# Mixer values normalized in the sample stage and streamed back by channel group

## The chip, the cores and the metric

The kernel runs on one core of a Trainium2 chip. The metric is the device time of one execution in microseconds (us), the median of several runs. PE is the matrix engine (TensorE), DVE the vector engine, ACT the scalar engine, POOL GpSimd, SP the engine that mostly issues DMAs. Each engine works through its own list of instructions in a fixed order, and waits where an operand or a buffer isn't ready.

## The reference, cut to what matters

One step of a two-layer decoder, for 1024 prompt tokens and a sample group of 64 tokens (8 sequences of 8) with 512 cached keys each. Layer 0 is what matters here:

```python
z = rms_norm(x, norm_g) @ w_in
zq, zk, zv, ga, zu, zvb, gb = jnp.split(z, cuts, axis=-1)
...
o_a = o.reshape(b, l, W_A) * jax.nn.silu(ga)                 # attention, gated
u = jax.nn.gelu(zu, approximate=False)
vb = layer_norm(jax.nn.gelu(zvb, approximate=False), ln_g, ln_b)
mixed = chunk_spatial(vb.reshape(b, l, G_B, CG_B), sp_w, sp_b).reshape(b, l, W_B)
o_b = u * mixed * jax.nn.silu(gb)                            # the mixer, gated
y = x + jnp.concatenate([o_a, o_b], axis=-1) @ w_out
```

`chunk_spatial` multiplies, for each of 8 channel groups of 128 and each chunk of 128 tokens, the values by a lower triangular 128x128 matrix over positions, and adds a bias per position. `layer_norm` is over the 1024 channels of a token: subtract the mean, multiply by the inverse deviation, by `ln_g` (per channel), add `ln_b` (per channel). The sample group's `vb` is an output. Layer 1 and the output projections aren't touched.

## The kernel before, in words

Tokens stand in 9 row tiles (8 of 128 prompt tokens, one of 64 sample tokens), or, transposed, in three column chunks (`CH`: 384, 384 and 320 columns). A projection is three matmuls per product (high by high, low by high, high by low part of the operands; `mm3`, L148 to L150), eight contraction tiles each: 24 matmuls.

Four stages of layer 0 follow each other:

- The head attention of the prompt (0 to 516 us). Its tail (516 to 572 us) still holds the last head's work, and between it the first `NPRE` = 8 of 24 gate units.
- A gate unit `gate_a(h, n)` (L240 to L256) is one head and one column chunk: it loads the attention output `oTr` from the DRAM buffer `oT_d` (ACT's queue, L248), does 24 matmuls into the PSUM tile `ga`, tanh on ACT (L250), one DVE operation (L251), the product on POOL (L254), and stores the result back into `oT_d` (ACT's queue, L255).
- The sample stage (572 to 816 us) is the attention of the 8 sample sequences over cached pages: key page transposes `ktp` (L536), whose PSUM tiles are copied to `kT` by DVE and ACT in turn (L537), then scores `ssc`, `ap`, values `sop`, and `sot`. Between its steps stands a list called `fill`: 16 gate units, and then 36 units `vb_unit` (L610 to L623), which project the mixer's values (`zv`: 4 column groups by 9 row tiles), copy them out (`zs`) and store them in the DRAM buffer `vb_d`. Key pages have 2 PSUM buffers, value pages (`vp`) 6 SBUF buffers.
- The mixer stage (816 to 1036 us): 24 units `b_dense` (48 matmuls into `zu` and `gb`, then Gelu, tanh, and products), each followed `ML` = 5 units later by `b_mix` (3 matmuls `mx` of the values with the position matrix, an addition of the bias `sbc` on DVE at L759, and the product `ob`). In its first steps `vb_norm` (L705 to L723) loads each of the nine row tiles from `vb_d`, takes Gelu on ACT (L712), statistics on DVE (L717) and POOL (L135, L136: inverse deviation), and two DVE operations (L720, L721) that apply mean and `ln_g`, and deviation and `ln_b`. All nine tiles stay in SBUF.

The code is written stage by stage. A scheduler with a cost model then sets the order in which each engine finds its instructions; DMAs go out in the order in which their issuing engine finds them, and hold that engine's later work back while they wait.

Of the kernel before, what the change touches and what calls it, by code (L numbers as in the profile page):

```python
# [23 lines left out]
NT = 9  # L24
# [12 lines left out]
NPRE = 8  # L37
# [18 lines left out]
ML = 5  # L56
# [20 lines left out]
def hybrid_step(  # L77
# [31 lines left out]
    vb_d = dram.tile([T + NS, D], F32, name="vb_d")  # L109
    v_d = dram.tile([T, D], F32, name="v_d")  # L110
# [77 lines left out]
    if True:  # L188
# [53 lines left out]
        def gate_a(h, n, new):  # L242
            load_gate(h)
            wh, wl = Wg[h]
            c0, cw = CH[n]
            pw_ = min(cw, SEQ - c0)
            mp, oT, g2 = new(h, n)
            nc.scalar.dma_start(oT[:, :pw_], oT_d[h][:, c0:c0 + pw_])  # L248
            mm3(mp[:, :cw], [(wh[k], wl[k], xh[n][:, k, :], xl[n][:, k, :]) for k in range(KT)])
            act.activation(g2[:, :cw], mp[:, :cw], AF.Tanh, scale=0.5)  # L250
            dve.scalar_tensor_tensor(g2[:, :cw], g2[:, :cw], 1.0, mp[:, :cw], ALU.add, ALU.mult)  # L251
            if n == 2:
                pool.tensor_copy(g2s[:, h, :], g2[:, pw_:cw])
            pool.tensor_tensor(oT[:, :pw_], oT[:, :pw_], g2[:, :pw_], ALU.mult)  # L254
            nc.scalar.dma_start(oT_d[h][:, c0:c0 + pw_], oT[:, :pw_])  # L255
            load_gate(h + 1)  # L256
# [249 lines left out]
        with ExitStack() as p15:  # L506
# [108 lines left out]
            def vb_unit(c, i):  # L615
# [6 lines left out]
                if i == NT - 1:  # L622
                    load_vb(c + 1)  # L623

            fill = [lambda h=h, n=n: gate_a(h, n, gate_tiles) for h, n in du[NPRE:]]
            fill += [lambda c=c, i=i: vb_unit(c, i) for c in range(4) for i in range(NT)]
# [41 lines left out]
        with ExitStack() as p2:  # L668
            pb = p2.enter_context(tc.tile_pool(name="pb", bufs=1, reuse_waits="tile"))
            vb = [pb.tile([P, D], F32, name=f"vb{i}") for i in range(NT)]  # L670

            lng = pb.tile([P, D], F32, name="lng")
            lnb = pb.tile([P, D], F32, name="lnb")
            nc.sync.dma_start(lng, ln_v_g.broadcast_to([P, D]))
            nc.sync.dma_start(lnb, ln_v_b.broadcast_to([P, D]))
# [10 lines left out]
            def mix_setup():  # L686
                for hh in range(2):
# [3 lines left out]
                    dve.tensor_copy(wT[:, hh * 4:hh * 4 + 4, :].rearrange("p g t -> p (g t)"), tp)  # L691
                tp = ps2.tile([P, 512], F32, tag="t", name="bdp", bufs=2)
# [11 lines left out]

            def vb_norm(i):  # L705
                r = rows(i)
                nc.sync.dma_start(vb[i][:r], vb_d[i * P:i * P + r, :])
                if i == NT - 1:
                    vx = pb.tile([P, D], F32, tag="ob", name="vx", bufs=1)
                    nc.sync.dma_start(vx[:r], vb_d[T:, :])  # L710
                    dve.tensor_tensor(vb[i][:r], vb[i][:r], vx[:r], ALU.add)
                act.activation(vb[i][:r], vb[i][:r], AF.Gelu)  # L712
                bst = pb.tile([P, 2, 6], F32, tag="bst", name=f"bst{i}", bufs=2)
                mv = pb.tile([P, 2], F32, tag="mv", name=f"mv{i}", bufs=2)
                rv = pb.tile([P, 1], F32, tag="lrv", name=f"lrv{i}", bufs=2)
                for q in range(2):
                    dve.bn_stats(bst[:r, q, :], vb[i][:r, q * 512:(q + 1) * 512])  # L717
                dve.bn_aggr(mv[:r], bst[:r].rearrange("p a b -> p (a b)"))
                rsqrt(rv[:r], mv[:r, 1:2], 1, 1.0)
                dve.scalar_tensor_tensor(vb[i][:r], vb[i][:r], mv[:r, 0:1], lng[:r], ALU.subtract, ALU.mult)  # L720
                dve.scalar_tensor_tensor(vb[i][:r], vb[i][:r], rv[:r], lnb[:r], ALU.mult, ALU.add)  # L721
                if i == NT - 1:
                    nc.sync.dma_start(vb_sample.rearrange("e b t d -> (e b t) d"), vb[i][:r])  # L723
# [7 lines left out]
            def b_dense(g, n):  # L731
# [7 lines left out]
                u = pb.tile([P, 384], F32, tag="u", name=f"u{g}_{n}", bufs=7)  # L739
# [7 lines left out]
            def b_mix(g, n, u):  # L747
# [6 lines left out]
                for q in range(nfull):  # L754
                    pe.matmul(mx[:, q * P:(q + 1) * P], vb[n * 3 + q][:, g * P:(g + 1) * P], wT[:, g, :], start=True, stop=True)
                mxs = pb.tile([P, 384], F32, tag="mxs", name=f"mxs{g}_{n}", bufs=2)
                if n == 2:
                    pe.matmul(mx[:, 256:320], vb[NT - 1][:NS, g * P:(g + 1) * P], bd[:, g, :], start=True, stop=True)
                dve.tensor_tensor(mxs[:, :nfull * P].rearrange("p (c t) -> p c t", t=P),  # L759
                                  mx[:, :nfull * P].rearrange("p (c t) -> p c t", t=P),  # L760
                                  sbc[:, g, :][:, None, :].broadcast_to([P, nfull, P]), ALU.add)
                if n == 2:
                    dve.tensor_tensor(mxs[:, 256:320].rearrange("p (c t) -> p c t", t=8),
                                      mx[:, 256:320].rearrange("p (c t) -> p c t", t=8),
                                      sbc[:, g, 0:8][:, None, :].broadcast_to([P, NB, 8]), ALU.add)
# [4 lines left out]
            load_b(0)  # L770
            units = [(g, n) for g in range(KT) for n in range(len(CH))]
            us = {}
            mi = 0
            for s in range(len(units) + 1):
                if s < len(units):
                    us[s] = b_dense(*units[s])
                    if units[s][1] == 0:
                        load_b(units[s][0] + 1)
                if s == 1:
                    mix_setup()  # L780
                for i in range(2 * s, min(2 * s + 2, NT)):
                    vb_norm(i)
# [711 lines left out]
```

## Time and profile before

| | before |
|---|---|
| median of 3 runs | 1791.06 us (1790.74 to 1792.69) |
| the profiled execution | 1789.87 us, its span 1788.1 us |
| PE busy | 1742.9 us, 97% of the span |
| DVE, ACT, POOL busy | 1006.3, 754.5, 605.6 us |
| DMA moved | 211.55 MB, mean 118 GB/s |

The span is the time between the first and last instruction that the profiler saw; the profiled execution's own time has 1.8 us more around it. PE is the engine to follow: where it is busy all the time, an instruction less on another engine is worth nothing by itself, and where it stands still, the wait names what is late.

### The profile page before, as it was taken

Reading aid. Unit: us, or ns where it says so; the run is one execution under the profiler, and the core shown is the slowest. Engines: PE = TensorE matmul, PEld = TensorE weight load, DVE = VectorE, ACT = ScalarE, POOL = GpSimd, SP = SyncE. Lnnn points to the kernel's source line nnn. Section 1 sums busy time; section 2 is a strip of 40 time slices with the busy share of each in tenths; the row PEclk is TensorE's granted clock in tenths of the full one; section 3 lists DMA queues with packets and bytes.
Section 4 is the critical chain, followed back from the end, with each engine's and each line's share of the span. In section 5 each row is a group of like instructions: output and inputs, shape, how many; then the busy total and the mean of one; then the engine's idle time right before and its main releaser. Section 6 shows DMA issues by size and latency. Waiting matters only on the chain.

```text
span 1788.1 us, 31862 instructions
## 1 busy us (share of the span) xinstructions
PE 1742.9 (97%) x11437; PEld 1631.3 (91%) x11437; DVE 1006.3 (56%) x2231; ACT 754.5 (42%) x1934; POOL 605.6 (34%) x881
## 2 busy tenths in 40 slices
PE   8999999999999999999999999999899999998998
PEld 8898999999999888889999999999899999996777
DVE  6988988888892322324833442534265445667442
ACT  5666666665763222223222332423252334345241
POOL 5656655565653221011522100144012223235240
PEclk8999999999999999999999999999999999998999
DMA  7202211220223766747221362433134334438741
GB/s 212 59 20 75 68 42 45 68 67 19 67 71 121 244 218 216 242 142 221 72 77 60 109 188 74 134 94 92 59 121 144 101 119 125 129 116 264 239 127 71
DMA packets 223141, 211.55 MB, mean 118 GB/s; under 512 B 22253, under 2 KB 200982, under 8 KB 222982
## 3 DMA queue, kind: packets, MB, share of 16 engines
q1 hardware_dynamic: 203350, 194.29, 35.1%
q10 hardware_dynamic: 19632, 15.21, 2.8%
q8 instruction: 91, 1.49, 0.4%
q14 instruction: 68, 0.56, 0.1%
HBM read 151.29 MB, written 56.24 MB: 116 GB/s over the span
## 4 chain that ended last, share of the span: by engine, by line
PE 66%; DVE 15%; DMA 6%; ACT 5%; POOL 4%; issue 3%; SPq 0%; ACTq 0%; POOLq 0%; DVEq 0%
PE o L1371 5%; PE yo L148 3%; PE yo L150 3%; PE yo L149 3%; PE vg L148 3%; PE vg L149 3%; PE vg L150 3%; PE zv L148 2%; PE zu L148 2%; PE zv L149 2%; PE zv L150 2%; PE zu L150 2%; PE gb L148 2%; PE zu L149 2%; PE gb L149 2%
## 5 line engine op out<-in xcount | busy, mean ns | idle before, releaser
L409 ACT ACTIVATE p<-s,nm 128x256 f32<-128x256 f32 (+7 forms) x128 | 95.0, 747 | 44.5 <-DVE nm L406 26.1
L396 PE MATMUL s<-ks,qs 128*128 128x512 f32 (+3 forms) x384 | 95.6, 363 | 3.9 <-DVE ks L381 2.2
L92 ACT CAST qs<-qs 64x256 fp32r<-64x256 f32 x128 | 51.7, 404 | 83.5 <-DVE qs L378 77.6
L1118 POOL TENSOR_TENSOR e<-e,k 128x256 f32<-128x256 f32 (+1 forms) x50 | 42.2, 850 | 111.6 <-ACT e L1115 97.6
L396 PEld LDWEIGHTS s<-ks,qs 128*128 128x128 f32 x384 | 64.3, 189 | 14.3 <-ACT qs L92 3.8
L431 PE MATMUL o<-v,at 128*128 128x128 f32 x576 | 75.9, 277 | 1.4 <-ACT at L92 1.4
L136 POOL TENSOR_TENSOR s<-s,mhalf 128x4 f32<-128x4 f32 (+1 forms) x72 | 74.5, 1035 | 5.2
L335 POOL TENSOR_TENSOR sq<-qk 128x256 f32<-128x256 f32 (+1 forms) x72 | 47.8, 664 | 83.1 <-ACT qk L92 82.1
L431 PEld LDWEIGHTS o<-v,at 128*128 128x128 f32 x576 | 70.6, 192 | 4.0 <-ACT at L92 2.4
L834 DVE TENSOR_TENSOR yp<-yp,yo 128x384 f32<-128x384 f32 (+1 forms) x48 | 25.4, 530 | 75.6 <-ACT yp L833 41.7
L404 DVE TENSOR_REDUCE nm<-s 128x1 f32<-128x640 f32 (+3 forms) x64 | 65.2, 1019 | 1.1
L744 POOL TENSOR_TENSOR u<-u,th 128x384 f32<-128x384 f32 (+1 forms) x24 | 28.6, 1192 | 99.8 <-DVE th L743 99.3
L402 DVE TENSOR_TENSOR s<-s,tb 128x256 f32<-128x256 f32 (+1 forms) x128 | 52.5, 412 | 8.9 <-PE s L396 5.8
L415 DVE SCALAR_TENSOR_TENSOR p<-p,fac,p 128x128 f32<-128x128 f32 (+3 forms) x64 | 54.7, 854 | 1.6
L1371 PE MATMUL o<-w1h,oh 128*128 128x512 f32 x128 | 53.0, 414 | 1.2 <-ACT oh L1348 1.2
L92 ACT COPY at<-atp 128x512 f32<-128x512 f32 (+2 forms) x96 | 44.6, 480 | 14.7 <-PE atp L424 14.2
L1371 PE MATMUL o<-w1l,oh 128*128 128x512 f32 x128 | 50.8, 397 | 0.0
L1371 PE MATMUL o<-w1h,ol 128*128 128x512 f32 x128 | 50.3, 407 | 0.0
L743 DVE SCALAR_TENSOR_TENSOR th<-th,gb 128x384 f32<-128x384 f32 (+1 forms) x24 | 12.5, 526 | 65.3 <-ACT th L742 65.3
L424 PE MATMUL atp<-cf,p 128*128 128x128 f32 x288 | 46.7, 273 | 1.7 <-DVE p L415 1.4
L340 POOL TENSOR_TENSOR qk<-qk,s 128x256 f32<-128x256 f32 (+1 forms) x72 | 46.0, 638 | 4.5
L1115 ACT ACTIVATE e<-e 128x512 f32<-128x512 f32 (+1 forms) x50 | 31.1, 623 | 37.4 <-DVE e L1114 33.6
(819 smaller groups left out, 6344.2 us busy)
## 6 DMA issues: line engine op xcount, KB each, us to landing
kp<-in_cache_k SPq DMA_DIRECT2D x32, 512.0 KB
vp<-in_cache_v SPq DMA_DIRECT2D x32, 512.0 KB
or<-oT_d SPq DMA_DIRECT2D x16, 384.0 KB
vb_d<-zs SPq DMA_DIRECT2D x36, 128.0 KB
oT_d<-ob SPq DMA_DIRECT2D x8, 544.0 KB
gt<-g_d SPq DMA_DIRECT2D x34, 128.0 KB
xt<-in_x_prompt SPq DMA_DIRECT2D x8, 512.0 KB
out<-v ACTq DMA_DIRECT2D x64, 64.0 KB
```

The source lines that it names most:

```text
L92: act.activation(o, i_, AF.Copy, scale=scale) if scale is not None else act.copy(o, i_)
L136: pool.tensor_tensor(dst, dst, mhalf[:dst.shape[0], :n], ALU.pow)
L148: pe.matmul(out, lh, rh, start=(s == 0), stop=False)
L149: pe.matmul(out, lh, rl, start=False, stop=False)
L150: pe.matmul(out, ll, rh, start=False, stop=(s == n - 1))
L396: pe.matmul(sc[c][:, k0:k0 + w], qs[:, c, l], kts[h, j][:, c, :w], start=(l == 0), stop=(l == 1))
L402: dve.tensor_tensor(sc[c][:, lo:n], sc[c][:, lo:n], backwards(tb[:, h, 0:n - lo]), ALU.add)
L404: dve.tensor_reduce(nm[:, c:c + 1], sc[c][:, :n], axis=AX.X, op=ALU.max, negate=True)
L409: act.activation(pc[:, :n], sc[c][:, :n], AF.Exp, bias=nm[:, c:c + 1], accum_out=ss[:, c:c + 1])
L415: dve.scalar_tensor_tensor(pt[0][:, :n], pt[1][:, :n], fac, pt[0][:, :n], ALU.mult, ALU.add)
L431: pe.matmul(op[:, :P], at[:, j * P:(j + 1) * P], vts[h, j], start=(j == 0), stop=(j == i))
L1371: pe.matmul(it.mp[:r], lh[:, k, :r], rh[k][:, cs], start=(k == 0 and a == 0), stop=(k == KT - 1 and a == 2))
```

## The change

- `NPRE` is 9: one gate unit more, (2,2), stands in the attention's tail.
- In `fill` the 36 `vb_unit` stand first, and the remaining 15 gate units behind them. Between these, after the third to the eleventh, stand nine `vb_norm`, in the sample stage now. A norm loads its row tile into the buffers of the value pages (tag `vp`, 6 for both), does Gelu, statistics and one DVE operation (subtract the mean, times the deviation; no `ln_g`, no `ln_b`), and stores the tile into a new DRAM buffer `vbn_d`. For the sample tile POOL also applies `ln_g` and `ln_b` for the output `vb_sample` (`vsout`).
- In the mixer stage the values are loaded from `vbn_d` by channel group, one group ahead (`load_vs`, two buffers). `ln_g` is applied where the position mix is read out of PSUM (`mxs`, now `mx * ln_g + sbc`), and `ln_b` is folded into `sbc` once (two matmuls of a matrix of ones with `wT`, eight DVE operations).
- `ML` is 2, and `u` has 4 buffers for 7. The weights of gate head 3 load after the last `vb_unit`.

```diff
-NPRE = 8
+NPRE = 9
-ML = 5
+ML = 2
...
+            def vb_norm(i):
+                r = rows(i)
+                vt = pb.tile([P, D], F32, tag="vp", name=f"vbn{i}", bufs=6)
+                nc.sync.dma_start(vt[:r], vb_d[i * P:i * P + r, :])
...
+                act.activation(vt[:r], vt[:r], AF.Gelu)
...
+                rsqrt(rv[:r], mv[:r, 1:2], 1, 1.0)
+                dve.tensor_scalar(vt[:r], vt[:r], mv[:r, 0:1], rv[:r], ALU.subtract, ALU.mult)
+                nc.sync.dma_start(vbn_d[i * P:i * P + r, :], vt[:r])
+                if i == NT - 1:
...
+                    pool.tensor_tensor(vs[:r], vt[:r], lnt[0][:r], ALU.mult)
+                    pool.tensor_tensor(vs[:r], vs[:r], lnt[1][:r], ALU.add)
+                    nc.sync.dma_start(vb_sample.rearrange("e b t d -> (e b t) d"), vs[:r])
+
+            fill = [lambda c=c, i=i: vb_unit(c, i) for c in range(4) for i in range(NT)]
+            for q, (h, n) in enumerate(du[NPRE:]):
+                fill.append(lambda h=h, n=n: gate_a(h, n, gate_tiles))
+                if 1 < q < NT + 2:
+                    fill.append(lambda i=q - 2: vb_norm(i))
...
+                    vs = vss[g] = pb.tile([P, NT, P], F32, tag="vs", name=f"vs{g}", bufs=2)
+                    nc.sync.dma_start(vs[:, :NT - 1, :], vbn_d[0:SEQ, g * P:(g + 1) * P].rearrange("(i p) d -> p i d", p=P))
+                    nc.sync.dma_start(vs[:NS, NT - 1, :], vbn_d[SEQ:T, g * P:(g + 1) * P])
...
+                for hh in range(2):
+                    tp = ps2.tile([P, 512], F32, tag="t", name=f"wsp{hh}", bufs=2)
+                    pe.matmul(tp, ones, wT[:, hh * 4:hh * 4 + 4, :], start=True, stop=True)
+                    for g in range(hh * 4, hh * 4 + 4):
+                        dve.scalar_tensor_tensor(sbc[:, g, :], tp[:, g % 4 * P:(g % 4 + 1) * P], lnc[1][:, g:g + 1], sbc[:, g, :],
+                                                 ALU.mult, ALU.add)
...
-                dve.scalar_tensor_tensor(vb[i][:r], vb[i][:r], mv[:r, 0:1], lng[:r], ALU.subtract, ALU.mult)
-                dve.scalar_tensor_tensor(vb[i][:r], vb[i][:r], rv[:r], lnb[:r], ALU.mult, ALU.add)
```

The order of the instructions moves at three places. The first is ACT at the beginning of the sample stage. Before, gate loads and stores (`oTr`, `oT_d`) stand around the first key copies `kT`:

```order
L255 DMA oT_d<-oTr_2_7898 128x256
L250 ACTIVATE g_3_0_7932<-ga_0_7930 128x384
L248 DMA oTr_1_8006<-oT_d 128x384
L255 DMA oT_d<-oTr_0_7931 128x384
L250 ACTIVATE g_3_1_8007<-ga_1_8005 128x384
L248 DMA oTr_2_8061<-oT_d 128x256
L537 COPY kT_1_7981<-ktp_0_1_7988 128x4x128
L179 CAST wg6h_8345<-wg6r_8344 128x384
L255 DMA oT_d<-oTr_1_8006 128x384
```

And now (`wv1h` is a weight tile of the value projection, `otp` the last head's output transposes, `zs` the copies of `zv`):

```order
L180 CAST wv1h_8358<-wv1r_8357 128x256
L251 ACTIVATE g_2_2_7853<-ga_2_7851 128x320
L92 ACTIVATE oT_7541<-otp_6_7884,sg 128x128
L92 ACTIVATE oT_7541<-otp_7_7887,sg 128x128
L256 DMA oT_d<-oTr_2_7852 128x256
L552 DMA vn_8422<-vsm 8x1024
L249 DMA oTr_0_10273<-oT_d 128x384
L622 COPY zs_1_8014<-zv_1_7989 128x256
L249 DMA oTr_1_10415<-oT_d 128x384
L622 COPY zs_3_8118<-zv_3_8093 128x256
L539 COPY kT_1_8018<-ktp_0_1_8025 128x4x128
```

The two gate loads there are of tiles whose buffers are free; no gate store stands between the key copies any more, and the first `zv` has the casts, one tanh and two copies ahead of it.

The second place is the end of the sample stage. Before, ACT has there the copies of the last `zv` and the small stores `osT`:

```order
L573 COPY sat_11067<-ap_11071 128x512
L620 COPY zs_1_11102<-zv_1_11077 128x256
L600 ACTIVATE osT<-sot_11105,sg 128x4x8 x2
L588 ACTIVATE ssq_11160,sms_11161<-sop_11138 128x128 x2
L620 COPY zs_3_11192<-zv_3_11167 128x256
L620 COPY zs_5_11248<-zv_5_11223 128x256
```

Now the last gates and norms (`vbn_11160` is row tile 6, `vbn_11228` row tile 7):

```order
L637 ACTIVATE vbn_11160<-vbn_11160 128x1024
L251 ACTIVATE g_6_1_11272<-ga_1_11270 128x384
L249 DMA oTr_2_11327<-oT_d 128x256
L180 CAST wb0h_11523<-wb0r_11522 128x256
L602 ACTIVATE osT<-sot_11173,sg 128x4x8 x2
L256 DMA oT_d<-oTr_1_11271 128x384
L590 ACTIVATE ssq_11263,sms_11264<-sop_11241 128x128 x2
L180 CAST wb0h_11529<-wb0r_11528 128x256
L637 ACTIVATE vbn_11228<-vbn_11228 128x1024
L180 CAST wb0h_11535<-wb0r_11534 128x256
L251 ACTIVATE g_6_2_11328<-ga_2_11326 128x320
```

On SP, in the same stretch, norm loads and stores follow the last value page (`vbn_10911`, `10990`, `11104`, `11160`, `11228` are row tiles 3 to 7):

```order
L527 DMA vp_3_11061<-in_cache_v 128x1024
L178 DMA wb0r_11528<-in_w_in 128x2x128
L178 DMA wb0r_11534<-in_w_in 128x2x128
L646 DMA vbn_d<-vbn_10911 128x1024
L178 DMA wb0r_11540<-in_w_in 128x2x128
L632 DMA vbn_11104<-vb_d 128x1024
L646 DMA vbn_d<-vbn_10990 128x1024
L632 DMA vbn_11160<-vb_d 128x1024
L646 DMA vbn_d<-vbn_11104 128x1024
L632 DMA vbn_11228<-vb_d 128x1024
```

The tile of a norm takes the buffer of the norm two before it, so its load stands behind that one's store; and the Gelu of row tile 7 stands on ACT ahead of the tanh of gate (6,2).

The third place is where the mixer stage begins, again on ACT. Before, it is reached from casts and norms:

```order
L179 CAST wb0h_11427<-wb0r_11426 128x256
L179 CAST wb1h_11489<-wb1r_11488 128x256
L179 CAST wb1h_11495<-wb1r_11494 128x256
L712 ACT_TABLE_LOAD
L712 ACTIVATE vb_11357<-vb_11357 128x1024
L712 ACTIVATE vb_11358<-vb_11358 128x1024
L740 ACTIVATE u_0_11482<-zu_0_11432 128x384
```

Now from the last two gate units, (7,1) and (7,2):

```order
L251 ACTIVATE g_7_1_11398<-ga_1_11396 128x384
L180 CAST wb0h_11541<-wb0r_11540 128x256
L180 CAST wb0h_11547<-wb0r_11546 128x256
L180 CAST wb1h_11612<-wb1r_11611 128x256
L249 DMA oTr_2_11429<-oT_d 128x256
L256 DMA oT_d<-oTr_1_11397 128x384
L251 ACTIVATE g_7_2_11430<-ga_2_11428 128x320
L256 DMA oT_d<-oTr_2_11429 128x256
L608 DMA oT_d<-osT 128x64 x8
L765 ACTIVATE u_0_11605<-zu_0_11555 128x384
```

The tanh of the last gate, (7,2), stands behind the store of gate (7,1), and the norms are gone from the mixer stage.

## Rows read from the trace of the kernel before

**Rows 1.** Windows by stage; columns: window, length, busy (instructions) by engine, PE clock, DMA share, GB/s

```profile
516.00:572.30 56.30, 53.87 (x352) 51.45 (x351) 30.46 (x64) 29.91 (x82) 21.78 (x36) 1.00 0.34 108
572.30:658.40 86.10, 82.43 (x583) 76.80 (x582) 25.39 (x49) 22.63 (x53) 21.20 (x29) 0.96 0.70 231
815.90:1036.00 220.10, 220.10 (x1372) 218.07 (x1371) 114.77 (x208) 67.06 (x141) 60.90 (x70) 1.00 0.37 115
```

**Rows 2.** Waits of PE from 505 to 1040 us: total, times, longest

```profile
PE ktp L536 <- ACT kT L537: 3.7, 1, 3.7
...
PE ga L148 <- ACT oT L92: 0.5, 1, 0.5
```

**Rows 3.** Window right after that wait, columns as in group 1

```profile
588.90:596.00 7.10, 7.01 (x26) 7.00 (x27) 2.05 (x4) 2.09 (x6) 1.93 (x3) 0.57 0.79 254
```

**Rows 4.** ACT's instructions around the wait: start, duration, instruction, idle before

```profile
582.03 0.33 ACTq L248 DMA_DIRECT2D oTr<-oT_d  x1
582.48 0.37 ACTq L255 DMA_DIRECT2D oT_d<-oTr  x1
...
587.98 0.33 ACTq L248 DMA_DIRECT2D oTr<-oT_d  x1
588.35 0.59 ACT L537 COPY kT<-ktp 128x512 f32<-128x512 f32 x1 [4.91 <-DMA oT_d<-oTr]
```

**Rows 5.** POOL's product that waited for the load issued at 582.03

```profile
586.25 0.99 POOL L254 TENSOR_TENSOR oTr<-oTr,g 128x384 f32<-128x384 f32 x1 [6.87 <-DMA oTr<-oT_d]
```

**Rows 6.** PE's prices by start times: mix matmuls, and a mixer unit between two of them

```profile
921.87 0.83 PE L755 MATMUL mx<-wT,vb 128*128 128x128 f32 x6
922.45 0.42 PE L148 MATMUL zu<-xh,wb4h 128*128 128x384 f32 x1
...
930.88 0.61 PE L755 MATMUL mx<-wT,vb 128*128 128x128 f32 x4
```

**Rows 7.** ACT at the border of attention and sample stage, where gates and copies meet

```profile
568.25 0.88 ACT L92 ACTIVATE oT<-otp,sg 128x128 f32<-128x128 f32 x3
...
573.98 0.44 ACT L250 ACTIVATE g<-ga 128x320 f32<-128x320 f32 x1 [2.01 <-DMA oT_d<-oTr]
...
574.37 0.41 ACT L179 CAST wg5h<-wg5r 128x256 fp32r<-128x256 f32 x1
```

**Rows 8.** DVE behind that tanh

```profile
574.51 0.49 DVE L251 SCALAR_TENSOR_TENSOR g<-g,ga 128x320 f32<-128x320 f32 x1 [2.91 <-ACT g L250]
```

**Rows 9.** Groups of the mixer stage by line and shape: busy, mean ns, idle before

```profile
L744 POOL TENSOR_TENSOR u<-u,th 128x384 f32<-128x384 f32 x16 | 21.1, 1323 | 88.3 <-DVE th L743 88.2
...
L720 DVE SCALAR_TENSOR_TENSOR vb<-vb,mv,lng 128x1024 f32<-128x1024 f32 x8 | 10.2, 1274 | 0.0
L717 DVE BATCH_NORM_STATS2 bst<-vb 128x6 f32<-128x512 f32 x16 | 10.1, 669 | 2.2 <-ACT vb L712 2.2
...
L712 ACT ACTIVATE vb<-vb 128x1024 f32<-128x1024 f32 x8 | 8.3, 1068 | 0.0
...
L136 POOL TENSOR_TENSOR lrv<-lrv,mhalf 128x1 f32<-128x1 f32 x8 | 6.7, 842 | 0.7
L135 POOL TENSOR_SCALAR lrv<-mv 128x1 f32<-128x1 f32 x8 | 5.8, 729 | 16.9 <-DVE mv L718 16.5
```

**Rows 10.** ACT's table load for the norms, same view

```profile
L712 ACT ACT_TABLE_LOAD x1 | 1.3, 1283 | 0.8 <-DMA vb<-vb_d 0.8
```

**Rows 11.** ACT's queue at low DMA load: a gate's store, and the load that waits for it

```profile
548.65 0.33 ACTq L255 DMA_DIRECT2D oT_d<-oTr  x1
550.81 0.33 ACTq L248 DMA_DIRECT2D oTr<-oT_d  x1
```

**Rows 12.** A window of high DMA load, columns as in group 1

```profile
644.00:648.00 4.00, 4.00 (x27) 3.96 (x27) 1.37 (x5) 1.22 (x4) 0.00 (x0) 1.00 1.02 403
```

**Rows 13.** PE's instructions of one sample sequence: values, scores

```profile
686.41 1.93 PE L583 MATMUL sop<-vp,sat 128*32 128x256 f32 x32
...
688.84 1.92 PE L547 MATMUL ssc<-kT,qbd 128*32 128x512 f32 x16
```

More of the change, by code (lines that the diff above doesn't have):

```diff
@@ L109, in hybrid_step @@
     vb_d = dram.tile([T + NS, D], F32, name="vb_d")
+    vbn_d = dram.tile([T, D], F32, name="vbn_d")
     v_d = dram.tile([T, D], F32, name="v_d")
@@ L255, in gate_a @@
             nc.scalar.dma_start(oT_d[h][:, c0:c0 + pw_], oT[:, :pw_])
-            load_gate(h + 1)
+            if h + 1 != NPRE // len(CH):
+                load_gate(h + 1)
         with ExitStack() as p1:
@@ L669, in hybrid_step, with load_vs @@
             pb = p2.enter_context(tc.tile_pool(name="pb", bufs=1, reuse_waits="tile"))
[L670 to L675, printed above, removed]
+            lnc = [pb.tile([P, KT], F32, name=f"lnc{q}") for q in range(2)]
+            nc.sync.dma_start(lnc[0], ln_v_g.rearrange("o (g p) -> p (o g)", p=P))
+            nc.sync.dma_start(lnc[1], ln_v_b.rearrange("o (g p) -> p (o g)", p=P))
+            vss = {}
+            def load_vs(g):
+                if g < KT and g not in vss:
+                    vs = vss[g] = pb.tile([P, NT, P], F32, tag="vs", name=f"vs{g}", bufs=2)
+                    nc.sync.dma_start(vs[:, :NT - 1, :], vbn_d[0:SEQ, g * P:(g + 1) * P].rearrange("(i p) d -> p i d", p=P))
+                    nc.sync.dma_start(vs[:NS, NT - 1, :], vbn_d[SEQ:T, g * P:(g + 1) * P])
             wT = pb.tile([P, H, P], F32, name="wT")
@@ L754, in b_mix @@
                 for q in range(nfull):
[L755 removed]
+                    pe.matmul(mx[:, q * P:(q + 1) * P], vss[g][:, n * 3 + q, :], wT[:, g, :], start=True, stop=True)
                 mxs = pb.tile([P, 384], F32, tag="mxs", name=f"mxs{g}_{n}", bufs=2)
                 if n == 2:
[L758 to L761, printed above, removed]
+                    pe.matmul(mx[:, 256:320], vss[g][:NS, NT - 1, :], bd[:, g, :], start=True, stop=True)
+                dve.scalar_tensor_tensor(mxs[:, :nfull * P].rearrange("p (c t) -> p c t", t=P),
+                                         mx[:, :nfull * P].rearrange("p (c t) -> p c t", t=P), lnc[0][:, g:g + 1],
+                                         sbc[:, g, :][:, None, :].broadcast_to([P, nfull, P]), ALU.mult, ALU.add)
                 if n == 2:
[L763 to L765 removed]
+                    dve.scalar_tensor_tensor(mxs[:, 256:320].rearrange("p (c t) -> p c t", t=8),
+                                             mx[:, 256:320].rearrange("p (c t) -> p c t", t=8), lnc[0][:, g:g + 1],
+                                             sbc[:, g, 0:8][:, None, :].broadcast_to([P, NB, 8]), ALU.mult, ALU.add)
                 dve.scalar_tensor_tensor(ob[:, c0:c0 + cw], u[:, :cw], 0.5, mxs[:, :cw], ALU.mult, ALU.mult)
@@ L778, in hybrid_step @@
                         load_b(units[s][0] + 1)
+                        load_vs(units[s][0])
                 if s == 1:
                     mix_setup()
-                for i in range(2 * s, min(2 * s + 2, NT)):
-                    vb_norm(i)
                 n = 0
```

38 lines of the change are left out of this document (18 added, 20 removed).

## The prediction

> **What bounds the kernel now.** I first read the windows by stage [rows 1]. In the mixer stage, from which the change takes its DVE and ACT work, PE is busy for 220.10 of 220.10 us. So a norm less on DVE there can't shorten the stage: nothing waits for it. In the attention's tail PE lacks 2.4 us of 56.3, and in the gate part of the sample stage 3.7 us of 86.1; that part alone shows a lower granted clock (0.96). These two are where time can be had.
>
> Next the waits of PE around this place [rows 2]. One is large: 3.7 us before a key page transpose, for ACT's copy of the transpose before it. Another, 0.5 us, is that of a gate for the copies of the last head's output. Behind the large one the window [rows 3] shows PE busy for 7.01 of 7.10 us at a granted clock of 0.57 of full speed, the lower of its two levels (1.2 GHz) for most of it, after a stretch in which PE stood still. At full speed the same work takes 0.57 x 7.01 = 4.0 us, so the wait cost another 3.0 us. The place is worth 6.7 us.
>
> Then ACT's list there [rows 4]. The copy that PE waits for began at 588.35. Ahead of it in ACT's order stood a gate load (587.98), which waited for the store issued at 582.48 to land: 5.5 us for 192 KB. A load is no quicker: that of 582.03 let POOL begin at 586.25, 4.2 us on [rows 5]. So it isn't ACT's work that held PE up, but a DMA round trip in the middle of ACT's queue.
>
> **The change, part by part.**
>
> *Removed stall.* With the value projections first, no gate store stands among the first key copies; the two gate loads there go into free buffers. So the 3.7 us and the 3.0 us of half clock go, and the 0.5 us wait for the last head's copies changes its form (below): -7.2 us. What is late next there is the value projection's own weights and copies, with nothing in ACT's queue that waits for a landing.
>
> *Added matmuls.* Two f32 matmuls of 512 columns. Three of 128 columns take 922.45 - 921.87 = 0.58 us [rows 6], so 512 take 0.77, and both 1.55 us, in a stage in which every us of PE counts. The position mix has as many matmuls as before.
>
> *First border.* The first value projection takes over the PSUM bank that the last head's transposes used, so it waits for their two copies. Ahead of these stand on ACT a cast that waits for the last gate matmul (0.41), its tanh (0.44), and the copies (0.88 for three, so 0.59 for two) [rows 7]: 1.43 us, of which the two transposes on PE cover some 0.2 to 0.3. I take 1.2 us. The lower end is the old wait of 0.5 [rows 2]; the upper one adds that a tanh there waited 2.0 us for a store [rows 7]: 3.2.
>
> *Second border.* The mixer stage's first matmul waits for DVE's evacuation of the last gate (7,2), where before it followed a value unit whose copy was short and whose bank was not the last. Tanh 0.44 [rows 7] and DVE 0.49 [rows 8] with the handoffs make 1.2 us. The tanh stands on ACT behind the store of gate (7,1), and that behind POOL, which has the `vsout` product between two gate products. 1024 columns on POOL cost up to 1323 x 1024/384 = 3.5 us [rows 9], so the wait can grow to some 4; behind it on ACT are the small `osT` stores and the first Gelu of the mixer, with PSUM buffers to spare. The lower end is 0.9. I take 1.4, near the tanh and DVE rows, since gate (7,2) itself gives POOL 3.5 us.
>
> *Late gates and norms.* This is the part with the widest bounds. Work per norm: Gelu 1.07, statistics 2 x 0.67, POOL 0.73 + 0.84, the last DVE operation at the price of the one that stays alike, 1.27 [rows 9]: 5.25 us. None of it loads an engine near its limit: in the gate part DVE was busy 25, ACT 23, POOL 21 of 86 us [rows 1], and nine norms add some 24, 10 and 14. Five table loads on ACT stand against one (1.28 each [rows 10]); beside PE they are hidden too. What counts is a chain. Norm 5 loads into norm 3's buffer once that is stored, norm 7 into norm 5's, and the Gelu of norm 7 stands on ACT ahead of the tanh that frees the bank for gate (7,1). From the `sop` of the sample sequence behind which norm 3's Gelu stands, this chain has two norms (10.5), a Gelu (1.07), two table loads (2.6), tanh and DVE (0.9), and handoffs (an estimate, 1.4): 16.5 us, and two round trips R of a store and a load. PE has from there to gate (7,1) six gate units: a mixer unit of two times 24 matmuls takes 930.88 - 922.45 = 8.43 us [rows 6], so a gate 4.2, one of 320 columns 3.5: 4 x 4.2 + 2 x 3.5 = 23.8. Values and scores of a sequence add 3.9 [rows 13], and the page transposes and small matmuls, an estimate, 2.5: 30.2. PE is late by 2R - 14.
>
> R by the nearest rows: at low load (share 0.34 [rows 1]) a load that waited for a store followed it after 2.2 us [rows 11]. Two such are 4.4; the 320 KB by which a norm's tile is larger take 0.8 us each way at 403 GB/s [rows 12]: 6.0. At high load 4.2 + 5.5 [rows 4, 5] and the same 1.6: 11.3. The traffic there is high: 231 GB/s over 86 us [rows 1] is 19.9 MB, and the norms add 8.5 x 1.05 = 8.9, so some 28 MB and 325 GB/s, if it has as many pages as before. But the chain's round trips stand on SP behind the last value page, and there the pages' load falls away. I take R = 8.0, a little under the middle: PE is late by 2.0 us. The ends give 0 and 8.6.
>
> The Trainium skill, "DMA: Bandwidth & Descriptors", section "Anatomy of one DMA", gives about 2.0 us fixed and the bytes over 436 GB/s for one DMA; by it a tile of 512 KB takes an estimated 3.2 us each way, so the chain wouldn't be late, and the sum below would be 2.0 less. The traced 192 KB took 4.2 and 5.5 us where the rule gives 2.4, so under load the measurement decides against it.
>
> *Hidden, at nothing.* The reads of the values by group, a whole group ahead of use (3 units of 8.43, 25 us of PE): DMA share is 0.37 in that stage [rows 1]. The `mxs` operation on DVE, the same shape with one operand more; eight small ones for `sbc`. `ML` 2 and fewer `u` buffers: the values no longer come late, so the shorter distance only matters if the mix, one unit behind, waits for them. If that cover fails, the cost is at most one load's 6 us at the first group.
>
> *Sum.* -7.2 + 1.55 + 1.2 + 1.4 + 2.0 = -1.05 us. The profiled execution took 1789.87, 1.2 less than the median of 1791.06; so 1788.8, and as a median 1790.0 us.
>
> **Rivals.**
>
> 1. *Forecast, chance 0.36:* 1790.0. The old stall goes, two borders and a late norm take most of it back. Its own range is 1787 to 1794; the upper part is for a late norm that also costs the half clock once (3.0 us more). A wait of 0.5 us left the clock at 1.00 [rows 1, 2], the one of 3.7 did not [rows 3], and 2.0 lies between.
> 2. *Slower: norm round trips under load, 0.23.* R near 9.7, what the traced tiles took without an addition for size: PE is late by 2 x 9.7 - 14 = 5.4 us, and the clock falls as after the 3.7 us wait, 3.0 more. -7.2 + 4.15 + 8.4 = +5.35: 1796.4. For it speaks the traffic, against it that the pages end before. It decides from R = 9.3 on (+1.5 and the clock).
> 3. *The old stall comes back among the late gates, 0.11.* The key copies of the last sequences stand there among gate stores and loads in ACT's queue, as before. 6.7 us again, which gives the chain of norms its slack: -7.2 + 4.15 + 6.7 = +3.65: 1794.7. Against it: in the old order, with gates beside the key copies for 86 us, it came once.
> 4. *Faster, 0.30:* R at most 7, so no late norm, and both borders at their lower ends (0.5 and 0.9): -7.2 + 1.55 + 1.4 = -4.25: 1786.8. For it speaks that PE waits nowhere in the rest of the sample stage.
>
> That the mixer stage's relief gains nothing is in all four, since PE was never short there.
>
> **Numbers.** A change of under 0.2% (3.6 us) is not told from none. Faster by more, below 1787.5, is most of case 4: 0.30 with the lower edge of case 1. Slower by more, above 1794.6, is case 2 and half of case 3: 0.30 with the upper edge of case 1. The rest is 0.40. The range is 1785.5, with case 4 and a little, to 1798.5: case 2 with R up to 10.8 (2.2 us more). Beyond it stay the end of R at 11.3 and a failing cover.
>
> **What would show it.** In the profile after: no wait of `ktp` for `kT` near 589 us, and PE's clock at 1.00 in the first 100 us of the sample stage; a wait of the first `zv` for ACT's copies of about 1 us; one of the first `zu` for DVE of 1 to 2 us; PE's waits for the late `ga` of some 2 us in all, with ACT's Gelu idle before it until a norm's load; the mixer stage 1.5 us longer, PE without a gap. It is wrong if the mixer stage shows waits for `vs`, if a key copy waits for a gate's store among the late gates, or if the mixer stage becomes shorter.

## The result and the profile after

| | before | after |
|---|---|---|
| median | 1791.06 us (1789.43 to 1795.09, 5 runs) | 1806.95 us (1805.55 to 1814.08, 5 runs) |
| ratio to before | | 1.0098, 95% interval 1.0071 to 1.0126 |
| span of the profiled execution | 1788.1 us | 1804.7 us |
| PE busy | 1742.9 us | 1746.8 us |

The change makes the kernel 15.9 us slower, where 1.0 faster was forecast and the range ended at 1798.5. Of the 16.6 us by which the span grew, PE stands still for 12.7 (57.9 for 45.2 us) and is busy for 3.9 more. Of all executions named below, one of e4 ran at a mean granted clock of 0.85 and took 1903 us; it is left out of e4's time and ratio.

The windows by stage say where. First before, in which the first window goes to the first matmul of the mixer stage and the second to that of the output projection; columns as in [rows 1]:

```profile
571.00:817.90 246.90, 242.54 (x2131) 215.81 (x2131) 68.95 (x147) 65.09 (x178) 38.01 (x57) 0.99 0.62 206
817.90:1027.60 209.70, 209.70 (x1308) 207.69 (x1306) 106.56 (x193) 62.16 (x132) 60.03 (x69) 1.00 0.34 108
```

The same two after:

```profile
571.00:831.27 260.27, 244.91 (x2121) 214.53 (x2121) 96.83 (x192) 82.82 (x200) 49.92 (x74) 0.98 0.71 235
831.27:1043.00 211.73, 211.73 (x1310) 208.98 (x1310) 76.30 (x148) 49.68 (x115) 41.48 (x53) 1.00 0.34 100
```

The sample stage is 13.4 us longer, and PE's idle time in it goes from 4.4 to 15.4 us. The mixer stage lost 30 us of DVE work and 12 of ACT, and is 2.0 us longer: PE was busy throughout before, and is now, with two matmuls more. All behind it is 1.2 us longer (761.7 for 760.5), which isn't put down to the change: two kernels of the experiments with the same code there, e5 and e3, take 759.0 and 762.9.

PE's waits in the changed sample stage (total, times, longest), which answer to [rows 2]:

```profile
PE ktp L538 <- DMA kp<-in_cache_k: 6.7, 3, 3.6
PE ga L149 <- DVE g L252: 4.7, 1, 4.7
PE zu L149 <- DVE g L252: 2.6, 1, 2.6
PE zv L149 <- ACT oT L92: 1.0, 1, 1.0
```

The wait for the copy `kT` is gone, and with it the half clock of [rows 3]. In its place stand four others. Two are the borders that were forecast (1.0 and 2.6 us). The third is the late gate (7,1). The fourth, key pages that come late from DRAM, was in no part of the prediction. PE's timeline has the larger three (start, duration, and in brackets the wait and what ended it):

```profile
761.54 1.94 PE L538 MATMUL ktp<-cf,kp 128*128 128x128 f32 x8 [3.55 <-DMA kp<-in_cache_k]
...
818.97 0.69 PE L149 MATMUL ga<-xh,wg7h 128*128 128x384 f32 x1 [4.73 <-DVE g L252]
...
831.27 0.45 PE L149 MATMUL zu<-xh,wb0h 128*128 128x384 f32 x1 [2.57 <-DVE g L252]
```

At the first two the granted clock fell to the lower level (0.50 in the single microseconds of the trace); behind the third it stayed at 1.00. The windows of the changed kernel there:

```profile
761.00:764.00 3.00, 2.46 (x11) 2.49 (x12) 0.69 (x1) 0.48 (x1) 0.00 (x0) 0.57 1.00 400
818.00:823.00 5.00, 4.03 (x13) 4.03 (x14) 3.87 (x9) 1.90 (x4) 2.72 (x7) 0.51 0.95 268
```

Those at the lower level cost 0.43 x 2.46 = 1.1 and 0.49 x 4.03 = 2.0 us, and some 0.4 between 764 and 765: 3.5 us, about what the one old place cost (3.0).

*Why key pages are late.* SP's queue in the changed kernel, before the wait at 761.54 (start, duration, DMA):

```profile
751.26 0.34 SPq L646 DMA_DIRECT2D vbn_d<-vbn  x1
754.08 0.36 SPq L527 DMA_DIRECT2D vp<-in_cache_v  x1
754.68 1.31 SPq L520 DMA_DIRECT2D kp<-in_cache_k  x1
756.22 0.33 SPq L527 DMA_DIRECT2D vp<-in_cache_v  x1
```

The first row stores the tile of norm 0. The value page behind it takes the buffer of that tile, so it goes out when the store has landed, 2.8 us behind the store's issue (2.3 of them SP stands there), and the key page, which needs no such buffer, stands behind it in order. Beside it go three more pages and two norm loads within 4 us, and it lands at 761.4, 6.7 us after its issue. Of the 6.7 us of key page waits, only this one, of 3.6, is behind a norm's store. One of 1.7 at 632 comes ahead of any norm, and one of 1.4 at 737 is for a page issued at 730.05, ahead of the first norm load (735.6).

*Why the late gate waits.* SP again: the store of norm 2, pages, the load of norm 3 (the fifth row) and, further down, the store of norm 5 and the load of norm 7:

```profile
777.64 0.34 SPq L646 DMA_DIRECT2D vbn_d<-vbn  x1
778.83 0.36 SPq L527 DMA_DIRECT2D vp<-in_cache_v  x1
779.43 0.34 SPq L520 DMA_DIRECT2D kp<-in_cache_k  x1
780.01 0.33 SPq L527 DMA_DIRECT2D vp<-in_cache_v  x1
781.12 0.33 SPq L632 DMA_DIRECT2D vbn<-vb_d  x1
...
807.47 0.32 SPq L646 DMA_DIRECT2D vbn_d<-vbn  x1
810.62 0.88 SPq L632 DMA_DIRECT2D vbn<-vb_d  x2
```

And ACT, with the step ahead of norm 3 that waited longest, the Gelu of norms 3 and 7, and the tanh of gate (6,2):

```profile
786.57 0.28 ACT L590 ACTIVATE ssq<-sop 128x128 f32<-128x128 f32 x1 [3.35 <-DMA kp<-in_cache_k]
...
789.35 1.06 ACT L637 ACTIVATE vbn<-vbn 128x1024 f32<-128x1024 f32 x1 [2.03 <-DMA vbn<-vb_d]
...
814.66 1.06 ACT L637 ACTIVATE vbn<-vbn 128x1024 f32<-128x1024 f32 x1 [2.46 <-DMA vbn<-vb_d]
...
815.92 0.43 ACT L251 ACTIVATE g<-ga 128x320 f32<-128x320 f32 x1
```

Norm 3's load went out only at 781.1. It waited for norm 2's store to land (3.5 us), so its tile takes norm 2's buffer, where those of norms 5 and 7 take that of the norm two before. It went fourth of six loads of 512 KB within 3.5 us, and took 8.2 us. ACT itself came to this Gelu only at 787.3, since a small load in its queue (`vn`, issued at 785.87) waited for a key page of the same burst to land; the last 2.0 us are the norm's load alone. Norm 5's store and norm 7's load took 3.15 and 4.0 us; the round trip before, norm 3's store and norm 5's load, took 7.6 together. Behind the tanh DVE had other work first:

```profile
815.75 1.29 DVE L642 BATCH_NORM_STATS2 bst<-vbn 128x6 f32<-128x512 f32 x2 [2.07 <-ACT vbn L637]
816.95 0.41 DVE L181 TENSOR_TENSOR wb0l<-wb0r,wb0h 128x256 fp32r<-128x256 f32 x1
817.30 1.22 DVE L636 TENSOR_TENSOR vbn<-vbn,vx 64x1024 f32<-64x1024 f32 x1
818.44 0.47 DVE L252 SCALAR_TENSOR_TENSOR g<-g,ga 128x320 f32<-128x320 f32 x1
```

The gate's own operation was free to go at 816.4 and came at 818.4, behind three operations of norms and weights.

### The profile page after: what moved, and what is told of

The parts are those of the page before. It is cut to its first block, busy times and chain, and to the rows that moved or that the text cites. A ratio compares the mean times of both kernels' runs of the same rounds, so it can differ in the third digit from the quotient of the medians.

```text
span 1804.7 us, 31938 instructions
## 1 busy us (share of the span) xinstructions
PE 1746.8 (97%) x11441; PEld 1629.2 (90%) x11441; DVE 1008.3 (56%) x2230; ACT 759.6 (42%) x1938; POOL 599.9 (33%) x883
## 4 chain that ended last, share of the span: by engine, by line
PE 45%; DMA 4%; DVE 2%; ACT 1%; issue 1%; SPq 0%; POOL 0%; DVEq 0%; ACTq 0%; POOLq 0%
PE o L1396 5%; PE yo L149 3%; PE yo L151 3%; PE yo L150 3%; PE vg L149 3%; PE vg L150 3%; PE vg L151 3%; PE zu L149 2%; PE gb L150 2%; PE zu L150 2%; PE zu L151 2%; PE gb L151 2%; PE gb L149 2%; PE qk L151 1%; PE qk L149 1%
## 5 line engine op out<-in xcount | busy, mean ns | idle before, releaser
L769 POOL TENSOR_TENSOR u<-u,th 128x384 f32<-128x384 f32 (+1 forms) x24 | 23.8, 990 | 143.7 <-DVE th L768 143.7
L768 DVE SCALAR_TENSOR_TENSOR th<-th,gb 128x384 f32<-128x384 f32 (+1 forms) x24 | 12.7, 530 | 96.9 <-ACT th L767 96.9
L765 ACT ACTIVATE u<-zu 128x384 f32<-128x384 f32 (+1 forms) x24 | 11.4, 474 | 95.9 <-PE zu L151 87.0
```

## The experiments

Each kernel was timed beside the kernel before on its chip, whose median lay between 1789.3 and 1790.5 us. Executions of one kernel spread over some 4 to 14 us, so kernels are compared by their ratios, and differences under 3 us between two of them are not taken as shown. Waits are those of one profiled execution of each; in e6 and e14 that was the slowest (1820.5 and 1811.3 us), in e10 the fastest (1802.2).

### The order alone, and the change without norms

e1 takes `before` and changes only `NPRE`, the order of `fill`, and where gate weights load:

```diff
-            fill = [lambda h=h, n=n: gate_a(h, n, gate_tiles) for h, n in du[NPRE:]]
-            fill += [lambda c=c, i=i: vb_unit(c, i) for c in range(4) for i in range(NT)]
+            fill = [lambda c=c, i=i: vb_unit(c, i) for c in range(4) for i in range(NT)]
+            fill += [lambda h=h, n=n: gate_a(h, n, gate_tiles) for h, n in du[NPRE:]]
```

> Only the new order of the sample stage: value projections first, gates behind them, nine gates in the attention's tail; the norms stay in the mixer stage as before, with all tiles kept in SBUF. Theory N (the norms' buffers and DMAs in the sample stage cost the time): the old stall of 3.7 us and its half clock (3.0) go, a first border of 1.0, a key page wait of 1.7 near 630 us and a second border of 1.2 come: about -3, so 1788 us, and no wait for late gates and none for key pages behind 700 us. Theory O (the order itself, with the gates beside the last pages, costs it): the key page waits of 5.0 us with their half clock and a wait among the late gates stay, the time is 1800 or more.

Measured: 1787.3 us against 1789.3, ratio 1.000 (0.9985 to 1.0014). Its waits in the sample stage:

```profile
PE zu L148 <- DVE g L251: 1.3, 1, 1.3
PE zv L148 <- ACT oT L92: 1.0, 1, 1.0
PE zv L148 <- ACT wv1h L179: 0.9, 1, 0.9
...
PE ktp L537 <- DMA kp<-in_cache_k: 0.4, 1, 0.4
```

The old stall is gone, the two borders are there with 1.0 and 1.3, late gates and key pages hardly wait, and the mixer stage with its norms takes 209.8 us. Theory O falls: the order doesn't cost the time. The gain of some 3 us that these waits add up to isn't clear of the spread either (2.0 us by the medians, nothing by the ratio).

e3 takes the changed kernel and leaves the norms out:

```diff
-                if 1 < q < NT + 2:
-                    fill.append(lambda i=q - 2: vb_norm(i))
...
-                    nc.sync.dma_start(vs[:, :NT - 1, :], vbn_d[0:SEQ, g * P:(g + 1) * P].rearrange("(i p) d -> p i d", p=P))
+                    nc.sync.dma_start(vs[:, :NT - 1, :], vb_d[0:SEQ, g * P:(g + 1) * P].rearrange("(i p) d -> p i d", p=P))
```

> The changed kernel without the nine norms: the mixer streams the raw value projections, and Gelu, mean, deviation and the sample output of the values are left out. Theory N: from 1807 go the key page waits behind 700 us (1.4 + 3.6, half clock 1.5), the late gate's wait (4.7, half clock 1.9) and 1.4 of the second border's 2.6: about -14.5, so 1792 us. Theory O: only the late gate's wait goes, 1800 us.

Measured: 1789.7 us, ratio 1.000 (0.9983 to 1.0017); waits of 1.3 (`zu`), 1.0 (`zv`), and 0.2 for a key page. Its mixer stage takes 211.7 us, as long as in the changed kernel. So streaming by channel group costs nothing to be seen but the two added matmuls, and the norms in the sample stage cost some 17 us by the ratios. The order of the other parts is sound; the rest asks what it is in the norms.

### Pace, bytes, queue

The list `fill` is spread evenly over 43 page steps, so nine more entries make page steps follow each other faster. e9 is e3 with nine empty entries in the norms' places, e10 the changed kernel with each norm in its gate's entry:

```diff
+                    fill.append(lambda: None)            # e9, for vb_norm
...
+                def unit(h=h, n=n, i=q - 2):             # e10
+                    gate_a(h, n, gate_tiles)
+                    if 0 <= i < NT:
+                        vb_norm(i)
+                fill.append(unit)
```

> The changed kernel without the norms, as in the earlier experiment, but with nine empty entries in the list in the places of the norms: page steps then come as fast beside the late gates as in the changed kernel (60 entries over 43 steps, 0.87 gates a step, where 51 entries give 1.19). The mixer streams raw projections. If the pace is what makes key pages late (a page step then has some 5 us of PE work for 6.3), the key page waits behind 700 us stay, and the time is 1796 to 1800. If the norms' hold on the shared buffers makes them late, it is as without norms: 1790.

> The changed kernel with each norm in the same entry of the list as its gate, so that the pace of the pages is that of 51 entries; buffers stay shared. If pace is the cause, the key page waits behind 700 us go and the time is 1797 or less, with a late wait for the norms' chain. If the shared buffers are, they stay: 1805.

Measured: e9 1791.9 us (1.0017, 1.0004 to 1.0030), e10 1806.5 us (1.0100, 1.0079 to 1.0122). The key page waits of e9, and the second of the two:

```profile
PE ktp L538 <- DMA kp<-in_cache_k: 4.5, 2, 2.7
...
738.75 0.63 PE L538 MATMUL ktp<-cf,kp 128*128 128x128 f32 x4 [1.77 <-DMA kp<-in_cache_k]
```

The waits of e10:

```profile
PE zu L149 <- DVE g L252: 6.6, 1, 6.6
PE ga L149 <- DVE g L252: 3.8, 3, 2.1
PE ktp L538 <- DMA kp<-in_cache_k: 1.3, 1, 1.3
```

The pace does make key pages late without any norm: e9 waits 2.7 us at 631 and 1.8 at 739, where the changed kernel waits 1.7 and 1.4. So these two waits are not the norms'; what e9 lacks is the third, of 3.6 us at 761, with its half clock. Alone the pace is worth some 2 us, hardly clear of the spread. At the slower pace the key pages wait 1.3 us for 6.7, but the norms come later and hold the last gates and the border up for 10.4 us for 7.3. One wait took the place of the other, and the time stayed, so each of e10's two expectations was half right: the key page waits behind 700 us went, as pace would have it, and the time stayed, as the buffers would.

e8 has norms of an eighth of the width, so an eighth of the bytes and of the columns, in the same buffers:

```diff
-                nc.sync.dma_start(vt[:r], vb_d[i * P:i * P + r, :])
+                nc.sync.dma_start(vt[:r, :128], vb_d[i * P:i * P + r, :128])
...
-                nc.sync.dma_start(vbn_d[i * P:i * P + r, :], vt[:r])
+                nc.sync.dma_start(vbn_d[i * P:i * P + r, :128], vt[:r, :128])
```

> The changed kernel with norms of 128 columns in place of 1024, in the same order, with the same buffers and the same waits (the rest of each row is left out, and the mixer streams raw projections): each norm moves 64 KB for 512 each way and has an eighth of the engine work. If the shared buffers and the order of the queue cost the time by themselves, it stays at 1802 us or more, with key page waits behind 700 us. If it is the norms' bytes beside the pages and the gates' round trips, the waits go as without norms: 1791 to 1793.

Measured: 1802.1 us (1.0067, 1.0045 to 1.0089), key page waits of 5.4 us, `ga` 2.7, `zu` 2.6. By the ratios the bytes and the work of the norms are worth some 5 us, and the intervals of this kernel and the changed one overlap; the larger part then is what the norms wait for and hold, which no run takes away by itself.

e6 lets POOL issue the norms' DMAs, so that SP doesn't stand at them:

```diff
-                nc.sync.dma_start(vt[:r], vb_d[i * P:i * P + r, :])
+                nc.gpsimd.dma_start(vt[:r], vb_d[i * P:i * P + r, :])
...
-                nc.sync.dma_start(vbn_d[i * P:i * P + r, :], vt[:r])
+                nc.gpsimd.dma_start(vbn_d[i * P:i * P + r, :], vt[:r])
```

> The changed kernel with the norms' loads and stores issued by POOL, not by SP; the six buffers stay shared. If key pages come late because SP stands at a norm's store or load with key page loads behind it, the waits for key pages behind 700 us go (5.0 us and 1.5 of half clock), and POOL's gate products may come later by what the norms hold POOL back: 1800 us. If it is the shared buffers (a value page whose buffer a norm still holds, on SP, ahead of the key page), they stay: 1805 or more, since POOL is held back too.

Measured: 1811.5 us (1.0114, 1.0085 to 1.0143), key page waits of 9.1 us, as expected of the shared buffers. Taking the norms' DMAs off SP doesn't bring the pages earlier; POOL stands at them instead, so more isn't shown.

### Buffers and the norms' place

e5 splits the six shared buffers, e14 splits them in halves:

```diff
-                vp = pb.tile([P, D], F32, tag="vp", name=f"vp{b}_{g}", bufs=6)
+                vp = pb.tile([P, D], F32, tag="vp", name=f"vp{b}_{g}", bufs=4)     # e14: 3
...
-                vt = pb.tile([P, D], F32, tag="vp", name=f"vbn{i}", bufs=6)
+                vt = pb.tile([P, D], F32, tag="vbn", name=f"vbn{i}", bufs=2)       # e14: 3
```

> The changed kernel with the six buffers that value pages and norms share split into four for pages and two for norms. If key pages come late because a value page, ahead of them on SP, waits for a norm's tile to be stored, the waits for key pages behind 700 us go (5.0 us and 1.5 of half clock): 1800 us. If they come late because SP itself stands at a norm's store, or because of the traffic, they stay: 1806. Four page buffers may cost a wait of their own of 1 to 2 us.

> Three buffers for value pages and three for norms. If the number of norms in flight limits their pace (two buffers: 9 us a norm), three let them end earlier, and the time is at or below the 1796 of four and two. If value pages need their buffers (a sequence has four pages), three make pages late: waits for values (sop) or key pages of several us, 1800 or more.

Measured: e5 1795.8 us (1.0041, 1.0026 to 1.0056), e14 1806.6 us (1.0092, 1.0072 to 1.0113). e5 gives back about 10 us of 17, more than expected. Its waits for late gates are gone, key pages wait 3.3 us, 1.3 of them behind 700 us (at 738), and the wait at 761 is gone. SP's first norm load and the store of norm 7 in e5:

```profile
693.59 0.32 SPq L632 DMA_DIRECT2D vbn<-vb_d  x1
...
777.38 0.34 SPq L646 DMA_DIRECT2D vbn_d<-vbn  x1
```

In the changed kernel the first load goes out at 735.6. With buffers of their own the norms start 42 us earlier, beside the last projections, and eight of them are through 42 us before the stage's end. In e14 they are through earlier still (norm 7's store at 749.9), but pages are short: values wait for pages (`sop`) 3.8 us, and other steps of the sample sequences (`sot`, `an`) 8.1.

e4 has the shared buffers and norms two gates earlier in the list; e12 has the split buffers and each norm behind its row's last projection; e11 is the split with norms in their gates' entries:

```diff
-                if 1 < q < NT + 2:
-                    fill.append(lambda i=q - 2: vb_norm(i))
+                if q < NT:                                # e4
+                    fill.append(lambda i=q: vb_norm(i))
...
+            for i in range(NT):                           # e12
+                fill.insert(28 + 2 * i, lambda i=i: vb_norm(i))
```

> The changed kernel with each norm two gates earlier (norm i behind gate i, not gate i + 2). If the late gate waits for the chain of norms 3, 5 and 7, the chain now has two gates (8 us) more: that wait (4.7 us and 1.9 of half clock) goes, the key page waits stay or move to earlier pages: 1800 us. If that wait comes from the traffic at the stage's end as such, it stays and the time is 1806.

> Split buffers (four for value pages, two for norms), and each norm in the list right behind the last value projection of its row tile. If what matters is that the norms are through before the last gates (in the split kernel the first norm loads at 694 and all but the last are done by 778 us, where in the changed kernel they go from 736 to 822), this is as fast as the split or faster: 1792 to 1796. If norms beside the projections only move the waits to earlier key pages, it is 1800 or more.

> Both: four buffers for value pages and two for norms, and each norm in its gate's entry. If pace adds to the buffers, the time falls below the 1796 of the split alone: 1791 to 1793, with the second border (2.4) and the mixer's two matmuls (1.9) left over what the order alone gives. If pace is nothing, it stays at 1796.

Measured: e4 1803.7 us (1.0098, 1.0063 to 1.0134), e12 1797.9 us (1.0040, 1.0024 to 1.0057), e11 1803.1 us (1.0074, 1.0051 to 1.0097).

e4 has the norms earlier in the list and not in time: the first load goes out at 734.0. In both kernels it stands on SP among loads that wait for PE, so the list alone doesn't set its time. Gate (7,1) still waited 4.0 us, now for another reason; ACT in e4:

```profile
807.00 0.33 ACTq L256 DMA_DIRECT2D oT_d<-oTr  x1
...
813.13 0.39 ACTq L249 DMA_DIRECT2D oTr<-oT_d  x1
813.57 1.06 ACT L637 ACTIVATE vbn<-vbn 64x1024 f32<-64x1024 f32 x1 [4.61 <-DMA oT_d<-oTr]
814.53 0.41 ACT L251 ACTIVATE g<-ga 128x320 f32<-128x320 f32 x1
```

The gate load waited 6.1 us for a store, as in [rows 4], with the norm and the tanh behind it. e12 is like e5, with `ga` at 0.7 and `zu` at 0.2; it is no faster, though `zu` hardly waits at the border any more (`sot` does there, 1.2 us). e11 missed both expectations: its norms ran from 708 to a last store at 810, and its gates waited in four places, 4.9 us in all, and key pages in nine, 4.7 us. So buffers of their own help where the norms also end before the last gates; why e11's took so long stayed open.

### Gate buffers, and the two small additions

e15 gives the gates three attention tiles for two:

```diff
-                        pb.tile([P, 384], F32, tag="oT", name=f"oTr{h}_{n}", bufs=2),
+                        pb.tile([P, 384], F32, tag="oT", name=f"oTr{h}_{n}", bufs=3),
```

> The changed kernel with three buffers for the gates' attention tiles in place of two: a gate's load waits for the store three units before it, no longer two, so ACT's queue is held less by landings. If ACT's queue behind gate stores makes the late waits (with norms two gates earlier the last tanh stood 4.6 us behind such a store), the wait of gate (7,1) shrinks from 4.7 to 1 or 2 us and the time is 1800. If the norms' own chain makes it, it stays at 1806.

Measured: 1816.3 us (1.0162, 1.0132 to 1.0191): slower, which neither theory had. The late gate waits 6.7 us for 4.7, and key pages 8.7 for 6.7. The order moved too: the gate that waits is (7,0) here, and norm 7's Gelu, which waited for its load, stands ahead of the tanh of (6,1); ACT in e15:

```profile
815.49 1.06 ACT L637 ACTIVATE vbn<-vbn 128x1024 f32<-128x1024 f32 x1 [3.88 <-DMA vbn<-vb_d]
816.45 0.47 ACT L251 ACTIVATE g<-ga 128x384 f32<-128x384 f32 x1
```

So here too the norms' chain ends last, as in the changed kernel; ACT's gate queue did so only in e4, with the norms' places moved. Why e15 is slower than the changed kernel was not taken apart.

e7 drops the two `pool.tensor_tensor` for `vsout` and the loop with `wsp` from the changed kernel, and the loads of `ln_g` and `ln_b` for the former:

```diff
-                    pool.tensor_tensor(vs[:r], vt[:r], lnt[0][:r], ALU.mult)
-                    pool.tensor_tensor(vs[:r], vs[:r], lnt[1][:r], ALU.add)
...
-                    pe.matmul(tp, ones, wT[:, hh * 4:hh * 4 + 4, :], start=True, stop=True)
```

> The changed kernel without POOL's two operations for the sample output and without the two matmuls of ones and their eight DVE operations (ln_b is left out of the mix, ln_g and ln_b out of the sample output). The mixer stage goes from 211.7 to 209.8 us, as long as it was before, if these matmuls are all that the new mixer costs. The second border's wait goes from 2.6 to 1.3 us if POOL's work made it, and stays if ACT's queue of gate stores did. Together 1804 us, or 1805 with the border as it is. A wait among the late gates stays in both.

Measured: 1805.7 us (1.0079, 1.0051 to 1.0107). The border's wait was 2.0 us for 2.6. That POOL's work makes a part of it is not shown: e15, with that work, waits 1.9. Behind e7's wait the clock was 0.83 over 9.8 us, 1.7 us lost; the mixer stage took 211.5, so 209.8 without that, as before.

## Why the prediction was wrong

- *The old stall:* right by the traces. It is gone in the changed kernel and in e1, with its half clock: -7.2 us. e1's times alone don't show so much.
- *First border:* right, 1.0 us for 1.2. *Second border:* 2.6 for 1.4, within its bounds. *Added matmuls:* 2.0 us of mixer stage for 1.55. It is theirs: the stage takes 211.7 with them (e3, without norms) and 209.8 without (e1, with the norms still in it). The price had been scaled up from matmuls of 128 columns; the two of 512 took 1.02 us each:

```profile
852.15 1.02 PE L733 MATMUL wsp<-wT,ones 128*128 128x512 f32 x2
```

- *Late gates and norms* is the step that failed. The size of R was right: 7.6 and 7.15 us for 8.0. But the prediction let the chain start with norm 3's Gelu right behind the sample sequence's `sop` (779.2). The Gelu came at 789.4: its load had waited for norm 2's store and then took 8.2 us among pages, and ACT stood behind a key page of the same burst. And the chain ended with a tanh and one DVE operation, where DVE had 2 us of other work ahead. From `sop` to the gate it took 39.8 us, where 16.5 and two R of 8.0 made 32.5. PE's own work up to there was priced too low as well, 34.7 us for 30.2 (a second sequence's values, at 805.62, lie on the way), and by luck this hid over half of the error. So PE was late by 4.7 us, and 2.0 of half clock, for 2.0 in all.
- The same step had the page loads "fall away" ahead of the norms, and asked of the shared buffers only which norm waits for which. It did not ask which *page* waits for a norm, and put late key pages at nothing; no rival had them. They wait 6.7 us for 0.7 before, and cost 1.5 of half clock. Of this the 3.6 us at 761 and the half clock go with the norms in shared buffers: e9 (no norms), e5 (buffers of their own) and e10 (slower pace) lack that wait. The other 3.1 go with the faster pace of the page steps (e9), which the prediction didn't price either.
- *The mixer's relief gains nothing:* right; its 30 us of DVE work were beside a PE that was always busy.
- *Rival 2* (slower, 1796.4) had the late chain with its half clock, near its size (6.7 for 8.4 us), but by round trips of 9.7 us, which didn't come: its size is right by luck. *Rival 3* did not come: no key copy holds PE up in the changed kernel. Stalls of its kind are in e8 (a key copy, 1.5 us) and in e4 (at a gate).
- None of the three signs that the prediction named for being wrong came either. It looked for them in the mixer stage and at key copies, and not at key pages.

By parts: -7.2 (old stall) + 1.0 and 2.6 (borders) + 2.0 (matmuls) + 6.7 (late gate, 4.7 and 2.0 of clock) + 7.5 (key pages, 6.7 - 0.7 and 1.5 of clock) = +12.6 of the span's 16.6 us. The rest (1.2 behind the mixer stage, some 3 in busy time and small waits ahead of it) isn't assigned to a part of the change.

The norms as a whole are what costs (e1, e3). Shown is the part that goes with buffers of their own and an earlier end (e5 and e12, 10 us each by the ratios). Bytes and engine work (e8, some 5 us) and the pace of the page steps (e9, some 2 us) are near the spread. These don't add up independently, since a wait that is taken away brings out the next (e10, e4). What keeps e5 and e12 some 7 us above e3 was not taken apart by a run. e5's trace has key page waits of 3.3 us for e3's 0.2, waits of `an` and `sot` of 2.6 for none, a second border of 2.4 for 1.3, and half clock at the start of a mixer stage of 214.2 us for 211.7. Two buffers for norms beside six for pages were not tried, so what four page buffers cost stays open.

The Trainium skill, "DMA: Bandwidth & Descriptors", section "Anatomy of one DMA — SWDGE (gpsimd) path", would give an estimated 3.2 us for each 512 KB; it is stated for DMAs that GpSimd issues, and those here are SP's. Norm 5's store took 3.15 us (DMA share 0.57) and is near it, norm 7's load 4.0 (0.85) is a quarter above, and norm 3's load, in a burst with pages (1.02), took 8.2. The one price fits the first alone.

## What to carry to other kernels

Before work is moved into a stage because its engines are idle there, ask which buffers it borrows and who waits for them: a ring that two streams share ties the faster one to the slower, and everything behind it in an in-order queue. Work that stood beside a fully busy engine was free where it was: nothing was won by taking it away (the mixer stage stayed at 209.8 us but for the added matmuls), and it had to be paid where the busy engine waits for DMAs. And price a chain from the moment when its first load can go out, not from the place where its first instruction stands.

## What the hardware showed that was not expected

Products on POOL slowed DVE beside them. DVE's weight operation of 128x256, 0.42 us by its median, took 1.15 us beside a gate product and 2.33 beside one for the sample output. DVE in the changed kernel:

```profile
826.83 1.15 DVE L181 TENSOR_TENSOR wb0l<-wb0r,wb0h 128x256 fp32r<-128x256 f32 x1 [0.46 <-ACT wb0h L180]
828.15 2.33 DVE L181 TENSOR_TENSOR wb0l<-wb0r,wb0h 128x256 fp32r<-128x256 f32 x1 [0.17 <-ACT wb0h L180]
```

And POOL there:

```profile
826.70 1.00 POOL L255 TENSOR_TENSOR oTr<-oTr,g 128x384 f32<-128x384 f32 x1
827.66 2.54 POOL L653 TENSOR_TENSOR vsout<-vsout,ln 64x1024 f32<-64x1024 f32 x1
```

Both end 0.3 us behind POOL's operation beside them. The Trainium skill, "SBUF — State Buffer", section "SBUF: two separate sides", has the two engines take a shared pair of ports for a whole instruction; these rows agree. The gate operation that ends the second border stood behind the longer one, some 0.8 us after its tanh was done; that this costs time is not shown (e7 against e15). Also, a wait's length alone didn't tell whether the granted clock falls: behind 2.0 us in e7 it was 0.83 over 9.8 us, behind 2.6 in the changed kernel 1.00. And the norm's last DVE operation with two scalars took 0.82 us at the median, where the one with a full operand had 1.27 [rows 9].
